# Attention scores with 128 queries of one head on half of TensorE's rows, a bias table of 128 rows, and experts' first matrices laid out anew, in a hybrid mixer and mixture-of-experts kernel

## The chip, the cores and the metric

The kernel runs on one core of one Trainium2 chip. The metric is the device time of one execution in microseconds (us). Below, PE is TensorE's matmuls and PEld its weight loads, DVE is VectorE, ACT ScalarE, POOL GpSimd and SP SyncE, on whose queue most DMAs are issued. A matmul holds a *stationary* operand in the array (loaded ahead of it) and streams a *moving* operand through it; the result goes to a bank of PSUM. In the rows, `64*64` or `128*128` behind a matmul's operands are the rows and columns of the array that it uses, and `64x512 f32` is the moving operand.

## What is computed

One layer of a decoder trunk on 512 tokens of 1024 channels, all in float32 at the ends. The normalised input goes through one projection; 256 channels go through a state-space mixer (S5), 256 through a multi-scale pooling, and 512 through causal attention with 8 heads of 64 channels and a relative bias; the three are joined, go through `w_out` and are added to x. Then each token is sent to two of 16 experts (first a group of four by its logits, then two in the group), and a last norm follows. Cut to what the change touches:

```python
s = einsum('bhqd,bhkd->bhqk', q, k) * dh**-0.5 + bias_t[:, t5_bucket(q_pos - k_pos)]
s = where(q_pos >= k_pos, s, NEG_INF);  out = softmax(s) @ v
x = x + concat([ssm, pool, att]) @ w_out
h = rms_norm(x);  comb = weights of the 2 experts of 16 that each token takes
hg = einsum('td,edf->tef', h, w_gate);  hu = einsum('td,edf->tef', h, w_up)
x = x + einsum('tef,efd->td', silu(hg) * hu * comb, w_down)
```

## The kernel before, in words

The tokens are 4 tiles `m` of 128 (`NT`), the heads 4 pairs `hp` of two (`NPAIR`). The program is written as Python generators (`s_attend`, `s_gather`, `unit_xt` and many more), each a stream of small stages. A stage ends with `yield engine, needs, tokens`: the next stage runs on that engine, after the events `needs`, and holds the `tokens` (buffers). A planner, the class `Flow`, has a cost for every instruction and takes at each step the ready stage that its own clock and the streams' ranks put first. So the order of the instructions on each engine is fixed while the program is built, and the diff does not show it. All instructions are recorded by one helper, so nearly every row of the profile has line L96, and tiles tell the instructions apart.

Attention (`s_attend`, line 1080). For each tile and pair, 64 queries at a time (`b` = 0, 1): two matmuls, one for each head `j`, give the scores `psS`, both into one bank of the tag "at" (there are two such banks), head 0 in partitions 0 to 63 and head 1 in 64 to 127. Then one chain of 128 rows (64 queries of two heads): DVE adds the bias table `tb` and takes the row maximum (`pr<-psS,tb`), ACT takes the exponential, DVE divides, PE transposes (`ptp`), ACT copies the result to `pts`. When both halves are there, `po` multiplies by the values. Scores of tile m have W = 128(m+1) columns.

The bias table `tb` has 64 distances for each of two heads on its 128 partitions, 4 pairs of 576 columns; it is read from a scratch array `t_scr` by 8 DMAs of 16 partitions each (`s_tscr`, near line 777), one long run of a shifted row each. The causal mask is in it.

Routing and experts. When `w_out` for a tile is done, `pth` transposes the normed tile, `pl` gives the router's logits, and DVE, ACT and PE (`pc`, counts of tokens per expert) find each token's slot. Tokens of the first unit of expert work are gathered by matmuls with a 0/1 matrix, `gb<-sel,xp` (`s_gather`, line 1417), whose stationary operand is a 128x128 part of the normed tokens; the other units read their tokens back from memory and transpose them (`tx`, `unit_xt`, line 1595). The 1024 channels are split into 8 parts as `(c k)`: part k takes every eighth channel, so neighbouring columns of an operand are 32 bytes apart. This matches the experts' weights in memory, where a partition holds 8 neighbouring rows. Expert weights arrive as float32, and ACT and DVE split each into two float16 halves (`gu` and `dn`); then `pg` (gate and up) and `py` (down) run on PE.

Of the kernel before, what the change touches and what calls it, by code (L numbers as in the profile page):

```python
# [19 lines left out]
P = 128  # L20
D = 1024
S = 512
# [14 lines left out]
TW = 576  # L37
VW = TW + HD - 1
# [65 lines left out]
class Flow:  # L104
# [176 lines left out]
def hybrid_trunk_kernel(tc, a, out, cap=CAPACITY, dbg=None):  # L281
# [93 lines left out]
    tb = ap_.tile([P, NPAIR, TW], F32, name="tb")  # L375
# [370 lines left out]
    def s_bias():  # L746
# [332 lines left out]
    def s_attend(tiles):  # L1079
        while tiles:  # L1080
            m, hp = tiles.pop(0)
            W = P * (m + 1)
            for b in range(2):
                qt = 2 * m + b
                yield "pe", (("q", hp), ("k", hp), "tb"), ("at",) if b else ("at", "pts")
                if b == 0:
                    pts = ap_.tile([P, NT, 2, P], F32, tag="pts", name=f"pts{m}_{hp}", bufs=2)
# [7 lines left out]
                one = lambda n: ap_.tile([P, 1], F32, tag=n, name=f"{n}{m}_{hp}_{b}", bufs=4)  # L1095
                yield "dve", (), ("pr",)
                pr = ap_.tile([P, S], F32, tag="pr", name=f"pr{m}_{hp}_{b}", bufs=3)
                mx, nm, sm_, rcp = one("mx"), one("nm"), one("smx"), one("rcp")
                v.tensor_tensor_reduce(out=pr[:, 0:W], in0=psS[:, 0:W], in1=tb[:, hp, c0:c0 + W],
                                       scale=1.0, scalar=LOW, op0=ALU.add, op1=ALU.max, accum_out=mx)  # L1100
                fl.give("at")
                v.tensor_scalar(nm, mx, -1.0, None, ALU.mult)
                yield "act"
                act.activation(pr[:, 0:W], pr[:, 0:W], AF.Exp, bias=nm, accum_out=sm_)
                yield "dve"
                v.reciprocal(rcp, sm_)
                v.tensor_scalar(pr[:, 0:W], pr[:, 0:W], rcp, None, ALU.mult)
                yield "pe", (), ("tr",)
                pt = bank("tr", f"ptp{m}_{hp}_{b}")
                for kt_ in range(m + 1):  # L1110
                    pe.transpose(pt[:, kt_ * P:(kt_ + 1) * P], pr[:, kt_ * P:(kt_ + 1) * P], ident)
                fl.give("pr")
                yield "act"
                act.copy(pts[:, 0:m + 1, b, :], pt[:, 0:W].rearrange("p (k q) -> p k q", q=P))
                fl.give("tr")
            yield "pe", tuple(("v", hp // 2, t) for t in range(m + 1)), ("po",)
# [935 lines left out]
```

## Time and profile before

| | us |
|---|---|
| device time, median of 3 runs | 437.32 (436.31, 437.32, 441.03) |
| device time of the profiled run | 435.2 |
| its span | 433.2 |
| mean granted clock of TensorE, as a share | 0.951 |

| engine | busy us | share of the span | instructions |
|---|---|---|---|
| PE | 381.7 | 88% | 3336 |
| PEld (weight loads, beside PE) | 214.4 | 49% | 3336 |
| DVE | 321.1 | 74% | 650 |
| ACT | 236.3 | 55% | 400 |
| POOL | 50.7 | 12% | 86 |

The DMA queues moved 109.41 MB, 253 GB/s in the mean. A row of the timeline gives the start in us from the span's start, the time until the group's last end, engine, line, operation, output and inputs, and behind x the number of instructions in the group; in square brackets stands the idle time just before and what ended it. An f32 matmul is two records in the trace, so `x4` of `psS` are two matmuls.

### The profile page before, as it was taken

Reading aid. Unit: us, or ns where it says so; the run is one execution under the profiler, and the core shown is the slowest. Engines: PE = TensorE matmul, PEld = TensorE weight load, DVE = VectorE, ACT = ScalarE, POOL = GpSimd, SP = SyncE. Lnnn points to the kernel's source line nnn. Section 1 sums busy time; section 2 is a strip of 40 time slices with the busy share of each in tenths; the row PEclk is TensorE's granted clock in tenths of the full one; section 3 lists DMA queues with packets and bytes.
Section 4 is the critical chain, followed back from the end, with each engine's and each line's share of the span. In section 5 each row is a group of like instructions: output and inputs, shape, how many; then the busy total and the mean of one; then the engine's idle time right before and its main releaser. Section 6 shows DMA issues by size and latency. Waiting matters only on the chain. (4 is left out here: it accounts for less than half of the span.)

```text
span 433.2 us, 8564 instructions
## 1 busy us (share of the span) xinstructions
PE 381.7 (88%) x3336; PEld 214.4 (49%) x3336; DVE 321.1 (74%) x650; ACT 236.3 (55%) x400; POOL 50.7 (12%) x86
## 2 busy tenths in 40 slices
PE   2899896898999999999999989899998876678992
PEld 1698453453644465445565975455454432233440
DVE  2798969747368778886898657978888777886383
ACT  4754133335469577865861115846786756466231
POOL 1200003124000000000124620001110010000011
PEclk9999999899999999999999978999998996589997
DMA  8935599219928979765786896548999996989933
GB/s 278 353 109 159 163 162 372 103 23 107 289 93 259 392 252 331 270 219 182 226 308 245 301 422 201 209 132 297 357 378 352 390 309 258 330 277 326 391 131 148
DMA packets 48872, 109.41 MB, mean 253 GB/s; under 512 B 4508, under 2 KB 25756, under 8 KB 48829
## 3 DMA queue, kind: packets, MB, share of 16 engines
q1 hardware_dynamic: 45676, 99.15, 70.0%
q0 software_dynamic: 2592, 9.44, 5.4%
q10 hardware_dynamic: 560, 0.25, 0.4%
q8 instruction: 27, 0.44, 0.4%
q14 instruction: 17, 0.13, 0.1%
HBM read 84.13 MB, written 24.69 MB: 251 GB/s over the span
## 5 line engine op out<-in xcount | busy, mean ns | idle before, releaser
L96 PE MATMUL pg<-gu,xts 128*32 128x512 f16 (+1 forms) x960 | 71.4, 397 | 6.6 <-ACT gu L96 6.6
L96 DVE SCALAR_TENSOR_TENSOR gu<-st_lde,gu 128x1024 f16<-128x1024 f32 x56 | 67.4, 1219 | 11.0 <-ACT gu L96 10.6
L96 ACT ACTIVATE gu<-st_lde 128x1024 f16<-128x1024 f32 x56 | 58.0, 1057 | 18.0 <-DMA st_lde<-in_moe_w_up_dram 10.3
L96 PEld LDWEIGHTS <-xts 128*32 128x32 f16 (+1 forms) x960 | 31.0, 103 | 42.3 <-issue 16.8
L96 PE MATMUL py<-dn,aT 128*32 128x512 f16 (+1 forms) x480 | 40.9, 443 | 6.6 <-ACT aT L96 5.8
L96 PE MATMUL px<-wo,cat 128*128 128x512 f16 x192 | 44.5, 379 | 0.0
L96 DVE SCALAR_TENSOR_TENSOR dn<-st_lde,dn 128x1024 f16<-128x1024 f32 x32 | 38.5, 1220 | 6.3 <-ACT dn L96 6.1
L96 ACT ACTIVATE dn<-st_lde 128x1024 f16<-128x1024 f32 x32 | 33.4, 1058 | 4.3 <-DMA st_lde<-in_moe_w_down_dram 4.2
L96 PEld LDWEIGHTS <-hT 128*64 128x64 f16 (+1 forms) x384 | 31.3, 156 | 5.3 <-issue 1.2
L96 ACT ACTIVATE pr<-pr,nm 128x128 f32<-128x128 f32 (+3 forms) x32 | 17.9, 559 | 22.3 <-DVE nm L96 22.3
L96 PEld LDWEIGHTS <-aT 128*32 128x32 f16 (+1 forms) x480 | 15.3, 109 | 28.6 <-issue 8.9
L96 PEld LDWEIGHTS <-cat 128*128 128x128 f16 x192 | 18.2, 98 | 22.3 <-issue 3.6
L96 DVE CUSTOM_DVE_ANT_0 pr<-psS,tb 128x128 f32<-128x128 f32 (+3 forms) x32 | 15.6, 486 | 14.8 <-PE psS L96 14.7
L96 PE MATMUL ps_v<-w_v,hT 128*128 128x256 f16 x192 | 24.8, 290 | 0.9 <-ACT hT L96 0.5
L96 POOL DMA_INDIRECT y_scr<-ys,tok x10 | 10.5, 1047 | 124.2 <-ACT ys L96 124.2
L96 PE MATMUL psS<-qk 64*64 64x128 f32 (+3 forms) x128 | 23.3, 451 | 0.7 <-ACT qk L96 0.7
L96 PE MATMUL ps_k<-hT,w_k 128*128 128x512 f16 x96 | 22.5, 380 | 0.0
L96 PE MATMUL ps_q<-hT,w_q 128*128 128x512 f16 x96 | 22.2, 380 | 0.0
L96 ACT COPY pts<-ptp 128x128 f32<-128x128 f32 (+3 forms) x32 | 13.1, 422 | 15.4 <-PE ptp L96 15.4
L96 PE MATMUL ptp<-cpk,pr 128*128 128x128 f32 x80 | 14.4, 285 | 7.8 <-DVE pr L96 7.8
L96 POOL TENSOR_TENSOR sm_r<-ss 128x1 f32<-128x1 f32 x4 | 3.6, 901 | 123.0 <-ACT xs L96 123.0
L96 ACT ACTIVATE ys<-py,cw 128x512 f32<-128x512 f32 (+1 forms) x14 | 9.6, 686 | 15.2 <-PE py L96 13.5
(240 smaller groups left out, 653.8 us busy)
## 6 DMA issues: line engine op xcount, KB each, us to landing
st_lde<-in_moe_w_down_dram SPq DMA_DIRECT2D x32, 512.0 KB
st_lde<-in_moe_w_gate_dram SPq DMA_DIRECT2D x28, 512.0 KB
st_lde<-in_moe_w_up_dram SPq DMA_DIRECT2D x28, 512.0 KB
x_scr<-zero SPq DMA_DIRECT2D x12, 512.0 KB
xr<-x_scr SPq DMA_DIRECT2D x10, 512.0 KB
xp<-in_x_dram SPq DMA_DIRECT2D x8, 512.0 KB
y_scr<-zero SPq DMA_DIRECT2D x8, 512.0 KB
yr<-y_scr SPq DMA_DIRECT2D x4, 1024.0 KB
```

Source lines behind the costliest of these rows:

```text
L96: r = f(*args, **kw)
```

## The change

Three things are changed.

First, the scores. The two matmuls of a stage now take 128 queries of one head each, on the array rows of that head (64), all 128 columns, and each writes a bank of its own; the stage takes both "at" banks at once. Then two copies of a new generator `softmax`, one for each head, run the chain that was in the loop, 128 queries of one head each, and `po` waits for the event that the second signals. The number of score matmuls is halved; the chains' instructions keep their numbers and shapes. The planner's cost for a matmul on 64 rows gets a factor of 0.55.

Second, `tb` has 128 distances of one head on its partitions, 8 heads of 512 columns, and is again read by 8 DMAs of 16 partitions. Before, they read 512 runs of 2304 bytes (1.18 MB); now 1024 runs of 2048 bytes (2.10 MB).

Third, the host permutes the rows of the experts' gate and up matrices (`spread`), so that the channels can be split as `(k c)`, part k being 128 neighbouring channels. The loads of the matrices keep their form.

```diff
-TW = 576
-VW = TW + HD - 1
+TW = S
+VW = TW + P - 1
@@ planner's cost of a matmul
+            elif args[1].shape[0] == 64:
+                t *= 0.55
@@ the bias table
-    tb = ap_.tile([P, NPAIR, TW], F32, name="tb")
+    tb = ap_.tile([P, 2 * NPAIR, TW], F32, name="tb")
-        for j in range(2):
-            for r in range(0, HD, NC):
-                sp.dma_start(tb[j * HD + r:j * HD + r + NC], bass.AP(
-                    t_scr.tensor, t_scr.offset + j * NC * (VW + 1) + HD - 1 - r,
-                    [[VW, NC], [2 * NC * (VW + 1), NPAIR], [1, TW]]))
+        for r in range(0, P, NC):
+            sp.dma_start(tb[r:r + NC], bass.AP(
+                t_scr.tensor, t_scr.offset + P - 1 - r,
+                [[VW, NC], [NC * (VW + 1), 2 * NPAIR], [1, TW]]))
@@ s_attend
-            for b in range(2):
-                qt = 2 * m + b
-                yield "pe", (("q", hp), ("k", hp), "tb"), ("at",) if b else ("at", "pts")
...
-                psS = bank("at", f"psS{m}_{hp}_{b}")
-                for j in range(2):
-                    rows = slice(j * HD, (j + 1) * HD)
-                    pe.matmul(psS[rows, 0:W], qk[hp // 2][rows, 0, hp % 2, qt * HD:(qt + 1) * HD],
-                              qk[hp // 2][rows, 1, hp % 2, 0:W],
-                              start=True, stop=True)
-                c0 = 448 - HD * qt
...
+            yield "pe", (("q", hp), ("k", hp), "tb"), ("at", "at", "pts")
+            pts = ap_.tile([P, NT, 2, P], F32, tag="pts", name=f"pts{m}_{hp}", bufs=2)
+            pss = [bank("at", f"psS{m}_{hp}_{j}") for j in range(2)]
+            for j in range(2):
+                rows = slice(j * HD, (j + 1) * HD)
+                pe.matmul(pss[j][:, 0:W], qk[hp // 2][rows, 0, hp % 2, m * P:(m + 1) * P],
+                          qk[hp // 2][rows, 1, hp % 2, 0:W], start=True, stop=True)
+            c0 = TW - W
+            left = [2]
             for b in range(2):
+                fl.spawn(1, softmax(m, hp, b, pss[b], pts, c0, W, left))
+            yield "pe", (("pts", m, hp),) + tuple(("v", hp // 2, t) for t in range(m + 1)), ("po",)
...
-                              pts[:, kt_, :, j * HD:(j + 1) * HD],
+                              pts[:, kt_, j, :],
...
+    def softmax(m, hp, b, psS, pts, c0, W, left):
+        h = 2 * hp + b
...
+        v.tensor_tensor_reduce(out=pr[:, 0:W], in0=psS[:, 0:W], in1=tb[:, h, c0:c0 + W],
+                               scale=1.0, scalar=LOW, op0=ALU.add, op1=ALU.max, accum_out=mx)
+        fl.give("at")
...
+        left[0] -= 1
+        if not left[0]:
+            fl.sig(("pts", m, hp))
@@ s_gather (and the same line in unit_xt and in the path for crowded experts)
-        src = xs_m[m].rearrange("p (c k) -> p k c", k=KD)
+        src = xs_m[m].rearrange("p (k c) -> p k c", k=KD)
@@ host
+    def spread(w):
+        return np.ascontiguousarray(w.reshape(NE, KD, P, FE).transpose(0, 2, 1, 3)).reshape(NE, D, FE)
```

The planner's order moves with it. On PE, in the middle of the attention of pairs 0 and 1, before (`psS_1_1` are the scores of tile and pair's second half, `ptp` the transposes, `po` the product with the values, `pm` the pooling's matmul):

```order
L96 MATMUL ptp_1_0_1134<-cpk,pr_1_0_1089 128x128 x2
L96 MATMUL ptp_1_1_1137<-cpk,pr_1_1_1106 128x128
L96 MATMUL pm_1140<-scr_112,pw_sb 128x512
L96 MATMUL psS_1_1_1143<-qk_117 64x256 x2
L96 MATMUL po_1_1147<-pts_1_1034,v_sb 64x128 x2
L96 MATMUL psS_0_0_1151<-qk_117 64x384 x2
```

and at the same place after the change:

```order
L96 MATMUL po_0_1126<-pts_0_1020,v_sb 64x128 x4
L96 MATMUL ptp_1_0_1131<-cpk,pr_1_0_1084 128x128 x2
L96 MATMUL psS_0_0_1137<-qk_117 128x384
L96 MATMUL psS_0_1_1138<-qk_117 128x384
L96 MATMUL pm_1144<-scr_112,pw_sb 128x512
L96 MATMUL ptp_1_1_1160<-cpk,pr_1_1_1105 128x128 x2
```

The two matmuls of a stage (`x2` before) now stand as two rows with a bank each, next to each other, and the two transposes of a pair lie apart.

At the end of `w_out` for the last tile, on PE, before (`px` is `w_out`, `gb` the gather of two half units for a tile, `pth` the transposes for the router, `pc` the counts):

```order
L96 LDWEIGHTS cat_120
L96 MATMUL px_1_2563<-wo_1_2309,cat_120 128x512
L96 MATMUL gb_2652<-sel,xp_122 128x128 x4
L96 MATMUL gb_2653<-sel,xp_122 128x128 x4
L96 MATMUL pth_1_2676<-cpk,xp_123 128x128 x4
L96 LDWEIGHTS one_89
L96 MATMUL pc_2687<-base_87,one_89 128x16
```

and after:

```order
L96 LDWEIGHTS cat_120
L96 MATMUL px_1_2517<-wo_1_2322,cat_120 128x512
L96 MATMUL gb_2606<-sel,xp_122 128x128 x4
L96 MATMUL pth_1_2619<-cpk,xp_123 128x128 x4
L96 MATMUL gb_2607<-sel,xp_122 128x128 x4
L96 MATMUL gb_2606<-sel,xp_122 128x128 x4
L96 LDWEIGHTS one_89
L96 MATMUL pc_2655<-base_87,one_89 128x16
```

`pth` stands behind four gather matmuls where it stood behind eight, and four more come ahead of the counts. Somewhat later, at the last tile's logits `pl`, before:

```order
L96 MATMUL pc_2687<-hot,tri_88 128x16
L96 MATMUL gb_2652<-sel,xp_122 128x128 x4
L96 MATMUL pl_2708<-rw,h2T_2618 128x20 x8
L96 MATMUL gb_2653<-sel,xp_122 128x128 x4
L96 MATMUL gb_2652<-sel,xp_123 128x128 x4
L96 MATMUL gb_2653<-sel,xp_123 128x128 x4
L96 LDWEIGHTS one_89
L96 MATMUL pc_2762<-base_87,one_89 128x16
```

and after:

```order
L96 MATMUL pc_2655<-hot,tri_88 128x16
L96 MATMUL pl_2663<-rw,h2T_2573 128x20 x8
L96 MATMUL gb_2607<-sel,xp_122 128x128 x4
L96 MATMUL gb_2606<-sel,xp_123 128x128 x4
L96 MATMUL gb_2607<-sel,xp_123 128x128 x4
L96 LDWEIGHTS one_89
L96 MATMUL pc_2716<-base_87,one_89 128x16
```

The logits no longer stand behind a gather; the same three gathers lie between them and the last counts.

## Rows read from the trace of the kernel before

**Rows 1.** Windows by stage: stretch, its us, engines' busy time, clock, DMA share, GB/s

```profile
65.60:205.60 140.00, 131.98 (x879) 68.29 (x879) 101.97 (x246) 85.92 (x178) 13.83 (x16) 0.99 0.73 222
205.60:258.85 53.25, 50.56 (x296) 37.03 (x295) 40.40 (x138) 19.48 (x32) 17.81 (x33) 0.94 0.83 297
340.00:433.00 93.00, 68.60 (x638) 30.28 (x634) 63.24 (x85) 46.07 (x68) 6.41 (x9) 0.87 0.78 280
```

**Rows 2.** The tile of scores: ns of one (min/median/max), starts, forms

```profile
L96 PE MATMUL psS<-qk x128: 269/454/641, 65.7 to 198.6; 64*64 64x128 f32 x32, 64*64 64x256 f32 x32, 64*64 64x384 f32 x32, 64*64 64x512 f32 x32
```

**Rows 3.** Timeline of PE in the attention: scores, and other matmuls for comparison

```profile
97.92 0.86 PE L96 MATMUL psS<-qk 64*64 64x384 f32 x4
98.72 1.47 PE L96 MATMUL ps_p<-hT,w_p 128*128 128x512 f16 x6
...
119.25 1.08 PE L96 MATMUL psS<-qk 64*64 64x512 f32 x4
120.25 1.47 PE L96 MATMUL ps_q<-hT,w_q 128*128 128x512 f16 x6
...
126.29 1.88 PE L96 MATMUL pz<-xp,xs 128*128 128x512 f32 x4
128.10 1.08 PE L96 MATMUL psS<-qk 64*64 64x512 f32 x4
```

**Rows 4.** Timeline from the last tile's `w_out` to the first expert matmuls

```profile
237.82 3.89 PE L96 MATMUL gb<-sel,xp 128*128 128x128 f32 x16
238.66 0.68 DVE L96 SCALAR_TENSOR_TENSOR xp<-px,xp 128x512 f32<-128x512 f32 x1
241.55 0.60 PE L96 MATMUL pth<-cpk,xp 128*128 128x128 f32 x4
244.35 1.86 PE L96 MATMUL pl<-rw,h2T 128*128 128x20 f32 x16
249.49 0.23 DVE L96 TENSOR_SCALAR hot<-sm_r 128x16 f16<-128x16 f32 x1
252.05 0.18 PE L96 MATMUL pc<-base,one 1*128 1x16 f16 x1
254.83 4.09 PE L96 MATMUL gb<-sel,xs 128*128 128x128 f32 x16 [2.11 <-DVE sel L96]
258.85 5.36 PE L96 MATMUL pg<-gu,xts 128*32 128x512 f16 x96
```

**Rows 5.** Groups by line and form: f32 weight loads, busy us, mean ns of one

```profile
L96 PEld LDWEIGHTS gb<-sel,xp 128*128 128x128 f32 x48 | 11.8, 335 | 0.1
L96 PEld LDWEIGHTS tx<-cpk,xr 128*128 128x128 f32 x80 | 10.0, 194 | 5.8 <-issue 3.4 <-DVE xts L96 2.1 <-DVE dn L96 0.4
L96 PEld LDWEIGHTS ptp<-cpk,pr 128*128 128x128 f32 x80 | 9.3, 141 | 15.9 <-DVE pr L96 7.8 <-issue 5.1 <-ACT cat L96 0.7
...
L96 PEld LDWEIGHTS pl<-rw,h2T 128*128 128x128 f32 x64 | 7.6, 192 | 0.1
```

**Rows 6.** Timeline around the first use of the bias table

```profile
52.38 4.02 SPq L96 DMA_DIRECT2D tb<-t_scr  x8
...
69.91 0.28 DVE L96 CUSTOM_DVE_ANT_0 pr<-psS,tb 128x128 f32<-128x128 f32 x1
...
77.81 0.48 PE L96 MATMUL ptp<-cpk,pr 128*128 128x128 f32 x1 [4.70 <-DVE pr L96]
```

**Rows 7.** Windows, columns as in Rows 1, while the bias table loads and after

```profile
56.00:64.00 8.00, 8.00 (x97) 5.09 (x96) 5.30 (x5) 3.56 (x5) 0.00 (x0) 1.00 1.06 130
64.00:72.00 8.00, 7.31 (x39) 3.22 (x38) 7.96 (x13) 2.51 (x5) 0.35 (x2) 1.00 1.09 359
```

**Rows 8.** Page, part 5: score reductions and expert splits on DVE

```profile
L96 DVE SCALAR_TENSOR_TENSOR gu<-st_lde,gu 128x1024 f16<-128x1024 f32 x56 | 67.4, 1219 | 11.0 <-ACT gu L96 10.6
...
L96 DVE CUSTOM_DVE_ANT_0 pr<-psS,tb 128x128 f32<-128x128 f32 (+3 forms) x32 | 15.6, 486 | 14.8 <-PE psS L96 14.7
```

**Rows 9.** Timeline: the first split of later experts' weights

```profile
267.32 1.99 ACT L96 ACTIVATE gu<-raw 128x1024 f16<-128x1024 f32 x2
```

More of the change, by code (lines that the diff above doesn't have):

```diff
@@ L1082, in s_attend @@
             W = P * (m + 1)
-            for b in range(2):
-                qt = 2 * m + b
-                yield "pe", (("q", hp), ("k", hp), "tb"), ("at",) if b else ("at", "pts")
-                if b == 0:
-                    pts = ap_.tile([P, NT, 2, P], F32, tag="pts", name=f"pts{m}_{hp}", bufs=2)
-                psS = bank("at", f"psS{m}_{hp}_{b}")
-                for j in range(2):
-                    rows = slice(j * HD, (j + 1) * HD)
-                    pe.matmul(psS[rows, 0:W], qk[hp // 2][rows, 0, hp % 2, qt * HD:(qt + 1) * HD],
-                              qk[hp // 2][rows, 1, hp % 2, 0:W],
-                              start=True, stop=True)
-                c0 = 448 - HD * qt
[L1095 to L1115, printed above, removed]
@@ L1116, in s_attend @@
-            yield "pe", tuple(("v", hp // 2, t) for t in range(m + 1)), ("po",)
+            yield "pe", (("q", hp), ("k", hp), "tb"), ("at", "at", "pts")
[5 more added lines that the diff above has]
+                          qk[hp // 2][rows, 1, hp % 2, 0:W], start=True, stop=True)
@@ L1128, in s_attend @@
             fl.sig(("att", m, hp))
+    def softmax(m, hp, b, psS, pts, c0, W, left):
+        h = 2 * hp + b
+        one = lambda n: ap_.tile([P, 1], F32, tag=n, name=f"{n}{m}_{hp}_{b}", bufs=4)
+        yield "dve", (), ("pr",)
+        pr = ap_.tile([P, S], F32, tag="pr", name=f"pr{m}_{hp}_{b}", bufs=3)
+        mx, nm, sm_, rcp = one("mx"), one("nm"), one("smx"), one("rcp")
+        v.tensor_tensor_reduce(out=pr[:, 0:W], in0=psS[:, 0:W], in1=tb[:, h, c0:c0 + W],
+                               scale=1.0, scalar=LOW, op0=ALU.add, op1=ALU.max, accum_out=mx)
+        fl.give("at")
+        v.tensor_scalar(nm, mx, -1.0, None, ALU.mult)
+        yield "act"
+        act.activation(pr[:, 0:W], pr[:, 0:W], AF.Exp, bias=nm, accum_out=sm_)
+        yield "dve"
+        v.reciprocal(rcp, sm_)
+        v.tensor_scalar(pr[:, 0:W], pr[:, 0:W], rcp, None, ALU.mult)
+        yield "pe", (), ("tr",)
+        pt = bank("tr", f"ptp{m}_{hp}_{b}")
+        for kt_ in range(m + 1):
+            pe.transpose(pt[:, kt_ * P:(kt_ + 1) * P], pr[:, kt_ * P:(kt_ + 1) * P], ident)
+        fl.give("pr")
+        yield "act"
+        act.copy(pts[:, 0:m + 1, b, :], pt[:, 0:W].rearrange("p (k q) -> p k q", q=P))
+        fl.give("tr")
+        left[0] -= 1
+        if not left[0]:
+            fl.sig(("pts", m, hp))
     ATT = tuple(("att", m, hp) for m in range(NT) for hp in range(NPAIR))
@@ L1596, in unit_xt @@
         left = [2]
-        src = xr.rearrange("p (c k) -> p k c", k=KD)
+        src = xr.rearrange("p (k c) -> p k c", k=KD)
         for h in range(2):
@@ L1922, in hybrid_trunk_kernel @@
                     pt = psF.tile([P, 512], F32, tag="pf", name=f"pf{t}_{k}")
-                    pe.transpose(pt[:, 0:P], hs.rearrange("p (c k) -> p k c", k=KD)[:, k], ident)
+                    pe.transpose(pt[:, 0:P], hs.rearrange("p (k c) -> p k c", k=KD)[:, k], ident)
                     v.tensor_copy(hTf[:, k, t * P:(t + 1) * P], pt[:, 0:P])
@@ L1979, in layouts @@
          "w_in": f["w_in"].reshape(D, NPROJ), "w_out": f["w_out"].reshape(D, D),
-         "moe_w_gate": f["moe_w_gate"].reshape(NE, D, FE), "moe_w_up": f["moe_w_up"].reshape(NE, D, FE),
+         "moe_w_gate": spread(f["moe_w_gate"]), "moe_w_up": spread(f["moe_w_up"]),
          "moe_w_down": f["moe_w_down"].reshape(NE, FE, D)}
```

## The prediction, made before the change was run

> **What bounds the kernel now.** I read the windows by stage first, since a busy share over the whole span mixes stages with different limits. In [rows 1] the reader is to see PE's busy time against the length of each stretch. From the first scores (65.6 us) to the end of the attention's neighbourhood (205.6) PE is busy 131.98 of 140.00 us, 94%, at a clock of 0.99; from there to the first expert matmuls (258.85) it is busy 50.56 of 53.25, 95%. DVE and ACT have room in both. So up to 258.85 time taken out of PE's row of instructions moves everything behind it forward. In the last stretch PE is busy 68.60 of 93.00 us, so there it waits for something else, and a faster PE buys little. The chain of work that ended last covers only the last two microseconds and says nothing on this. Then I read the tile of the scores, the timeline of PE, and the groups by form.
>
> **A. Scores, in the first stretch.** There are 32 f32 records of each of four widths [rows 2]; four records are one stage (two matmuls of two records each), so 8 stages per width. From the start of a group to that of the next, four records of 384 columns take 98.72-97.92 = 0.80 us, and of 512 columns 120.25-119.25 = 1.00 us [rows 3]. The step of 0.20 per 128 columns gives 0.60 and 0.40 for the two smaller widths: (0.40+0.60+0.80+1.00) x 8 = 22.4 us in all. The change leaves 4 stages per width instead of 8, each with the same four records and the same moving columns.
>
> What does one stage then cost? Four records of 512 columns over the whole array (`pz`) take 128.10-126.29 = 1.81 us [rows 3], nearly twice the 1.00 of the scores. So the two heads' matmuls run side by side today. They use different rows and different columns of the array; after, they use different rows but the same columns, each with a bank of its own. If they still run side by side, the scores cost 22.4/2 = 11.2 and the change saves 11.2 us. If not, they go at the rate of `pz`: 1.81 x (1+2+3+4)/4 x 4 = 18.1, and it saves 4.3. No row shows two half-height matmuls over the same columns. The nearest is `psS` itself, whose heads differ in rows too, so I take the side near it: **10 us**, a little under the full gain since the weight loads are now 128 columns wide.
>
> **B. Gather and routing, in the second stretch.** The gather's stationary operand changes from every eighth channel to neighbouring ones. Its weight load takes 335 ns, where `pl`, of the same form from neighbouring elements, takes 192; among transposes, strided `tx` takes 194 and contiguous `ptp` 141 [rows 5]. So the stride lengthens a load. In `gb` the pace is 3.89/16 = 0.243 us a record, in `pl` 1.86/16 = 0.116 [rows 4]; a matmul of 128 moving columns alone needs 1.81/16 = 0.113 by `pz` [rows 3]. I take 0.12 us a record; 0.243 is the other bound (no gain). In `tx` the load grows by only 53 ns against `ptp`, and a load lies beside the matmul before it, so I count no gain there.
>
> Not all 64 records are on the path, so I follow it [rows 4]. `pth` starts at 241.55, behind 16 gather records; after, it stands behind 8, which end by 237.82+8x0.12 = 238.8, and its input is written by DVE at 238.66+0.68 = 239.34. So it starts near 239.4, 2.15 earlier, and the logits `pl` at 242.2 instead of 244.35. The one-hot `hot` ends at 249.72, 3.51 after the logits' end (246.21); now 242.2+1.86+3.51 = 247.57. The 24 gather records between now end by 247, so the counts `pc` start near 247.7 instead of 252.05: 4.35 earlier. The last gather follows 2.78 later, at 250.5, and its 16 records take 1.95 instead of 4.02, so the expert matmuls `pg` could start near 252.5 instead of 258.85. Their second half needs a cast behind the gather's end, which costs a few tenths. I take **6 us** (0 to 6.4).
>
> **C. The bias table.** It grows from 1.18 to 2.10 MB. While it loads, the DMA engines are fully busy (share 1.06) and move only 130 GB/s; once it is in, the same share moves 359 [rows 7]. At 130 GB/s, 2.10 MB take 16.1 us instead of 9.1. Its issues begin at 52.38; with a start-up of about 2 it then lands near 71, and its first reader starts at 69.91 [rows 6]. DVE is busy 7.96 of 8.00 us there [rows 7], so a late table delays it one for one, and PE, which already waits 4.70 us for DVE at 77.81 [rows 6], with it. The loads of projection weights behind the table come later as well. From below it costs 0 (it lands in time), from above the whole 7.0. I take **2.5 us lost**, since the estimate lies one to two microseconds behind the first use. [...]
>
> **D. Both score banks at once.** A stage now needs both "at" banks, so PE can't write a pair's scores while the other half is being reduced. DVE's 32 reductions take 486 ns in the mean, and DVE waits 14.7 us in all for PE's scores [rows 8]: today the scores, not the banks, are late. The bounds are 0 and one reduction for each of the 16 pairs, 16 x 0.486 = 7.8. I take **1 us lost**, since PE has other matmuls to run meanwhile.
>
> **E. What costs nothing.** Products with the values, transposes, exponentials and copies keep number and shape; a contiguous moving operand for `po` changes no row that I can find. The rows of the experts' matrices are permuted on the host, and their DMAs keep their form. What the late stage waits for are experts' weights. The splits of the weights that were loaded early begin at 267.32, with the first units of expert work [rows 9], and free the buffers of the next loads. These move forward with PE, so the gain should carry through; I add 0. If they did not, it would be swallowed, which is a rival below.
>
> **Sum.** 10 + 6 - 2.5 - 1 = 12.5 us. The profiled run took 435.2, so 422.7 by the same measure. The median of the runs is 2.1 above that run, so the forecast for the median is **425**.
>
> **The rivals.**
> 1. *The heads no longer run side by side.* Same columns of the array, so one after the other at the rate of `pz`: 4.3 + 6 - 3.5 = 6.8 us saved, about 430.5. Against it: the rows differ, as they do now.
> 2. *The end stage swallows it.* If the experts' weights arrive when they arrived before, because DMA sets their time (share 0.78 and 280 GB/s in the last stretch, where PE is idle a quarter of the time [rows 1]), the early gain turns into waiting: 435 to 438. Against it: the loads' buffers are freed by splits that start with PE's progress [rows 9].
> 3. *Slower: the pairs run in lockstep.* The chains of a pair start together, and the next scores need both banks. If each time the second reduction waits behind one weight split on DVE (1219 ns) and takes its own 486 ns [rows 8], and PE, its order fixed, stands still behind it, each of 16 pairs costs 1.7 us, 27 in all, against 16 saved less 2.5 by the table: 437.3+13.9 = about 451. It decides from (16-2.5)/16 = 0.84 us a pair on; the time is over 1% longer from 1.12. For it: DVE carries splits between the attention's instructions. Against it: DVE is busy only 102 of 140 us in that stretch [rows 1], and PE has projections and state-space matmuls between the pairs.
> 4. *Everything at its good end.* 11.2 + 6.4 and no loss: 17.6, so about 420.
>
> **How the numbers follow.** Forecast 0.58, rival 1 0.13, rival 2 0.15, rival 3 0.09, rival 4 0.05. The predicted time is that of the forecast. The range reaches down to 418, just under rival 4, and up to 434, over rival 1, and leaves out rivals 2 and 3 (0.24 together, of which the range's edge takes back a little). A change of 1%, 4.4 us, is about what a measurement of this kernel can tell from none. Forecast, rivals 1 and 4 are faster by more: 0.76, of which I give 0.02 to no change, since D and C together at their dear ends would eat rival 1; so faster 0.74, same 0.17 (rival 2 and this), slower 0.09.
>
> **What would show it.** A: four score records of 512 columns still take about 1.00 us from start to start, with 64 `psS` records instead of 128; if they take 1.8, rival 1 holds. B: `gb` at 0.12 us a record with a weight load near 192 ns, and from the last `pth` to the first `pg` about 13 us instead of 17.3. C: the first `pr<-psS,tb` one to three microseconds later against the scores ahead of it, with a wait for a DMA. D: no wait of PE's scores for DVE's reductions above some tenths; many of 1 to 2 us are rival 3. E: the distance from the first `pg` to the end unchanged at 433.2-258.85 = 174 us; if it grows by ten, rival 2 holds. I would be wrong above all if the planner's new order leaves PE waiting at places where it was fed before, which the rows of before can't show.

## The result, and the profile after

| | before | changed |
|---|---|---|
| device time, median of 20 runs, us | 437.45 | 432.8 |
| ratio to before, with its 95% interval | | 0.9889 (0.9864 to 0.9914) |
| span of the profiled run, us | 433.2 | 429.4 |
| mean granted clock of TensorE | 0.951 | 0.949 |

The change makes the kernel faster by 1.1%, 4.65 us between the medians. The forecast was 425, 12.4 us less than before: the sign is right, the size is not. Ratios, here and below, compare the fast runs alone, while times are medians of all runs, so the two can differ by some microseconds.

Four stretches tell where. The timeline of the changed kernel (start, us, engine, line, operation, output and inputs, idle time before):

```profile
73.81 0.29 DVE L96 CUSTOM_DVE_ANT_0 pr<-psS,tb 128x128 f32<-128x128 f32 x1 [3.79 <-DMA xs<-in_glu_w_dram]
...
81.37 0.28 DVE L96 TENSOR_SCALAR pr<-pr,rcp 128x128 f32<-128x128 f32 x1
...
81.71 0.48 PE L96 MATMUL ptp<-cpk,pr 128*128 128x128 f32 x1 [8.95 <-DVE pr L96]
...
88.80 0.70 PE L96 MATMUL psS<-qk 64*128 64x256 f32 x4
89.43 0.41 PE L96 MATMUL pk<-s1b,bbd 128*32 128x128 f32 x2
...
98.51 0.92 PE L96 MATMUL psS<-qk 64*128 64x384 f32 x4
99.35 1.13 PE L96 MATMUL pm<-scr,pw_sb 128*128 128x512 f32 x2
...
108.14 1.13 PE L96 MATMUL psS<-qk 64*128 64x512 f32 x4
109.20 0.55 PE L96 MATMUL ptp<-cpk,pr 128*128 128x128 f32 x3
...
207.01 0.59 PE L96 MATMUL px<-wo,cat 128*128 128x512 f16 x2 [1.77 <-ACT wo L96]
208.27 5.16 PE L96 MATMUL px<-wo,cat 128*128 128x512 f16 x16 [0.67 <-DVE wo L96]
...
236.01 1.05 PE L96 MATMUL gb<-sel,xp 128*128 128x128 f32 x8
236.97 0.66 PE L96 MATMUL pth<-cpk,xp 128*128 128x128 f32 x4
237.46 1.95 PE L96 MATMUL gb<-sel,xp 128*128 128x128 f32 x16
...
245.40 0.18 PE L96 MATMUL pc<-base,one 1*128 1x16 f16 x1
...
248.63 3.50 PE L96 MATMUL gb<-sel,xs 128*128 128x128 f32 x16 [2.56 <-DVE sel L96]
253.53 5.36 PE L96 MATMUL pg<-gu,xts 128*32 128x512 f16 x96 [1.40 <-DVE xts L96]
```

The first row's wait is for the bias table: the trace puts it down to another DMA, but with a faster table it is gone, and the kernel before with a larger table has the same wait with `tb` named (both below). The first scores start at 65.69 us, as before. From there:

| from ... to | before | changed | gain | forecast |
|---|---|---|---|---|
| first scores ... first transposes `ptp` | 77.81 [rows 6] | 81.71 | -3.9 | -2.5 (C) |
| ... first gather `gb` of the last block | 237.82 [rows 4], 160.0 later | 236.01, 154.3 later | 5.7 | 9 (A, D) |
| ... first expert matmul `pg` | 258.85 [rows 4], 21.0 later | 253.53, 17.5 later | 3.5 | 6 (B) |
| ... end | 433.2, 174.3 later | 429.4, 175.9 later | -1.5 | 0 (E) |
| sum | | | 3.8 | 12.5 |

Each of the four came out worse than forecast, and none by enough to explain the miss alone. The windows of the changed kernel (columns as in rows 1):

```profile
82.00:100.00 18.00, 18.00 (x106) 9.95 (x106) 11.94 (x44) 7.50 (x27) 3.20 (x4) 0.91 0.58 183
100.00:140.00 40.00, 38.19 (x294) 20.65 (x293) 27.55 (x65) 26.60 (x50) 6.31 (x6) 1.00 0.71 164
...
205.00:235.00 30.00, 27.56 (x162) 16.54 (x160) 21.12 (x68) 15.46 (x24) 8.76 (x16) 0.94 0.69 239
...
81.70:236.20 154.50, 148.87 (x968) 83.60 (x969) 112.91 (x300) 96.43 (x196) 18.27 (x26) 0.98 0.72 222
...
248.60:251.00 2.40, 2.37 (x12) 2.37 (x13) 1.88 (x8) 0.54 (x2) 1.85 (x4) 0.58 1.01 413
```

and of the kernel before, the stretches that answer to 81.70:236.20 and to the last gather:

```profile
77.80:238.00 160.20, 156.35 (x1028) 83.87 (x1028) 117.63 (x306) 99.95 (x199) 17.50 (x26) 0.99 0.71 218
...
254.80:258.90 4.10, 4.07 (x20) 3.95 (x24) 2.50 (x16) 0.81 (x2) 1.21 (x4) 0.61 1.02 417
```

PE has only 7.5 us less to do there (156.35 against 148.87), although the scores save 10 (below): the clock is 0.91 behind the wait for the table and 0.94 around the waits for `w_out`'s weights, and other matmuls take longer there. In 82:100 those of `ps_p` take 424 ns in the mean, in 205:235 those of `px` 401; in the same windows of before, at a clock of 1.00, they take 380 and 379. And it idles 5.6 us instead of 3.9; the waits for `w_out`'s weights, 1.77 and 0.67 us, do not stand in the trace of before.

### The profile page after: what moved, and what is told of

Same layout as the page of the kernel before. It is cut to its first block, busy times and chain, and to the rows that moved or that the text cites. A ratio compares the mean times of both kernels' runs of the same rounds, so it can differ in the third digit from the quotient of the medians.

```text
span 429.4 us, 8450 instructions
## 1 busy us (share of the span) xinstructions
PE 364.4 (85%) x3272; PEld 204.9 (48%) x3272; DVE 321.7 (75%) x649; ACT 236.1 (55%) x400; POOL 54.6 (13%) x87
## 4 chain that ended last, share of the span: by engine, by line
PE 50%; DMA 24%; DVE 13%; ACT 5%; issue 4%; SPq 1%; POOL 0%; POOLq 0%; ACTq 0%; DVEq 0%
PE px L96 7%; DMA st_lde<-in_moe_w_down_dram 7%; PE pg L96 6%; PE py L96 5%; DMA st_lde<-in_moe_w_gate_dram 4%; PE pf L96 4%; PE ps_v L96 4%; DVE gu L96 4%; DMA st_lde<-in_moe_w_up_dram 4%; DMA xs<-in_glu_w_dram 3%; PE psS L96 3%; PE pu L96 3%; PE ptp L96 3%; PE ps_k L96 3%; DVE dn L96 2%
## 5 line engine op out<-in xcount | busy, mean ns | idle before, releaser
L96 DVE SCALAR_TENSOR_TENSOR gu<-st_lde,gu 128x1024 f16<-128x1024 f32 x55 | 68.0, 1251 | 15.9 <-ACT gu L96 15.6
L96 PE MATMUL pg<-gu,xts 128*32 128x512 f16 (+1 forms) x960 | 71.7, 395 | 8.6 <-ACT gu L96 7.2
L96 ACT ACTIVATE gu<-st_lde 128x1024 f16<-128x1024 f32 x56 | 58.2, 1056 | 16.4 <-DMA st_lde<-in_moe_w_up_dram 11.1
L96 PEld LDWEIGHTS <-xts 128*32 128x32 f16 (+1 forms) x960 | 31.1, 103 | 44.0 <-issue 20.4
L96 PE MATMUL px<-wo,cat 128*128 128x512 f16 x192 | 45.6, 389 | 2.4 <-ACT wo L96 1.8
L96 PE MATMUL py<-dn,aT 128*32 128x512 f16 (+1 forms) x480 | 39.0, 420 | 8.8 <-ACT aT L96 7.5
L96 DVE SCALAR_TENSOR_TENSOR dn<-st_lde,dn 128x1024 f16<-128x1024 f32 x32 | 38.6, 1218 | 2.4 <-ACT dn L96 1.8
L96 ACT ACTIVATE dn<-st_lde 128x1024 f16<-128x1024 f32 x32 | 33.2, 1053 | 7.6 <-DMA st_lde<-in_moe_w_down_dram 7.5
L96 PEld LDWEIGHTS <-hT 128*64 128x64 f16 (+1 forms) x384 | 30.7, 155 | 5.1 <-issue 1.4
L96 PEld LDWEIGHTS <-cat 128*128 128x128 f16 x192 | 18.9, 100 | 24.3 <-issue 6.0
L96 PEld LDWEIGHTS <-aT 128*32 128x32 f16 (+1 forms) x480 | 14.8, 105 | 30.1 <-ACT aT L96 9.7
L96 ACT ACTIVATE pr<-pr,nm 128x128 f32<-128x128 f32 (+3 forms) x32 | 17.9, 562 | 15.0 <-DVE nm L96 14.8
L96 POOL DMA_INDIRECT y_scr<-ys,tok x10 | 11.9, 1190 | 103.9 <-ACT ys L96 78.6
L96 PE MATMUL ps_v<-w_v,hT 128*128 128x256 f16 x192 | 24.1, 282 | 1.0 <-ACT hT L96 0.6
L96 PE MATMUL ps_q<-hT,w_q 128*128 128x512 f16 x96 | 22.6, 380 | 0.0
L96 PE MATMUL ps_k<-hT,w_k 128*128 128x512 f16 x96 | 22.2, 380 | 0.0
L96 PE MATMUL ptp<-cpk,pr 128*128 128x128 f32 x80 | 13.6, 284 | 9.5 <-DVE pr L96 9.3
L96 DVE CUSTOM_DVE_ANT_0 pr<-psS,tb 128x128 f32<-128x128 f32 (+3 forms) x32 | 15.5, 485 | 7.7 <-DMA xs<-in_glu_w_dram 3.8
L96 ACT COPY pts<-ptp 128x128 f32<-128x128 f32 (+3 forms) x32 | 12.7, 424 | 12.5 <-PE ptp L96 12.4
L96 PEld LDWEIGHTS ptp<-cpk,pr 128*128 128x128 f32 x80 | 9.2, 141 | 17.4 <-DVE pr L96 9.4
L96 ACT ACTIVATE xs<-xp 128x512 f32<-128x512 f32 (+1 forms) x12 | 9.2, 770 | 14.5 <-DVE xp L96 10.7
L96 DVE TENSOR_TENSOR xts<-tx,xts 128x512 f16<-128x512 f32 x22 | 14.7, 685 | 2.4 <-ACT xts L96 2.1
```

What stands on the lines that cost most here:

```text
L96: r = f(*args, **kw)
```

## Experiments: the bias table

All ratios are to the kernel before, run on the same chip beside each of them. A difference to the changed kernel is given between the medians, which come from different chips, and in brackets by the ratios, where 1% is 4.4 us.

**The table on partitions 8 apart.** The same 2.10 MB in 1024 runs of the same length, but each DMA writes partitions r, r+8, r+16, ... instead of 16 neighbours. It reads each row from another of the 16 copies in `t_scr`, so the starts of its runs lie 2528 bytes apart instead of 2556:

```diff
-        for r in range(0, P, NC):
-            sp.dma_start(tb[r:r + NC], bass.AP(
+        for r in range(P // NC):
+            sp.dma_start(tb[r:P:P // NC], bass.AP(
                 t_scr.tensor, t_scr.offset + P - 1 - r,
-                [[VW, NC], [NC * (VW + 1), 2 * NPAIR], [1, TW]]))
+                [[VW + 1 - P // NC, NC], [NC * (VW + 1), 2 * NPAIR], [1, TW]]))
```

> The changed kernel with the same bias table, loaded by 8 DMAs of 16 partitions that lie 8 apart instead of side by side. Theory (the late table costs about 4 us, and the transfer is slow because 16 neighbouring partitions are written at a time): the first reduction of scores starts near 70 instead of 73.8, PE's wait for the first transposes falls from 8.95 to about 5 us, and the time falls by 3 to 4 us to a ratio of about 0.98 to before. Rival 1 (the partitions don't matter, the transfer is bound by the size or number of its runs): first reduction still near 73.8, ratio 0.989. Rival 2 (the table comes earlier but w_out's last weights still arrive near 207, so the gain is waited away): first reduction near 70, ratio 0.989.

Measured: 428.1 us, ratio 0.9788 (0.9752 to 0.9824), 4.7 us less than the changed kernel's median (4.4). Windows of each while the table loads, first the changed kernel, then this one:

```profile
56.00:60.00 4.00, 4.00 (x23) 2.29 (x22) 1.35 (x2) 2.98 (x4) 0.00 (x0) 1.00 1.10 128
60.00:64.00 4.00, 4.00 (x76) 2.79 (x75) 3.93 (x4) 0.59 (x1) 0.00 (x0) 1.00 1.07 124
```

```profile
56.00:60.00 4.00, 4.00 (x23) 2.29 (x22) 1.36 (x2) 2.97 (x4) 0.00 (x0) 1.00 1.06 205
60.00:64.00 4.00, 4.00 (x76) 2.79 (x75) 3.93 (x4) 0.59 (x1) 0.00 (x0) 1.00 1.08 207
```

and the timeline of this one:

```profile
69.92 0.28 DVE L96 CUSTOM_DVE_ANT_0 pr<-psS,tb 128x128 f32<-128x128 f32 x1
...
77.82 0.47 PE L96 MATMUL ptp<-cpk,pr 128*128 128x128 f32 x1 [5.07 <-DVE pr L96]
```

With the DMA engines as busy, 205 to 207 GB/s flow instead of 124 to 128. The first reduction starts at 69.92, as before the change (69.91, [rows 6]), and the first transposes at 77.82. The late table is thus real and costs 3.9 us at this place and 4.4 to 4.7 at the end. Both rivals of this run fall. The way from the one place to the other isn't shown: the traced execution is the longest of the five (433.6 us, the others 426 to 428), its mean clock is 0.936 where the changed kernel's is 0.949, and its gather starts at 237.83, later than the changed kernel's. Whether the partitions alone or also the other starts of the runs make the table faster was not tested apart.

**The larger table alone, in the kernel before.** Each run of a row is 1024 columns long instead of 576, of which the kernel uses 576; the planner counts the old size, so the order of all engines is that of before (one DMA of 2 KB more fills the end of `t_scr`):

```diff
-    tb = ap_.tile([P, NPAIR, TW], F32, name="tb")
+    tb = ap_.tile([P, NPAIR, 1024], F32, name="tb")
...
-                    [[VW, NC], [2 * NC * (VW + 1), NPAIR], [1, TW]]))
+                    [[VW, NC], [2 * NC * (VW + 1), NPAIR], [1, 1024]]))
```

> The kernel before with its own order and table, but 1024 instead of 576 columns loaded of each row (2.10 MB instead of 1.18, the rest of a row is not used). Theory (the larger table alone costs about 4 us and a lower clock behind the wait): first reduction of scores 3 to 4 us later, ratio about 1.01. Rival (the table's lateness is caught up later): first reduction later, ratio 1.00.

Measured: 440.4 us, ratio 1.006 (1.0015 to 1.0106), 2.5 us more. Its timeline:

```profile
74.07 0.29 DVE L96 CUSTOM_DVE_ANT_0 pr<-psS,tb 128x128 f32<-128x128 f32 x1 [3.88 <-DMA tb<-t_scr]
```

DVE waits 3.88 us, where the changed kernel waits 3.79, and 2.5 of it are left at the end. The larger table alone makes a kernel slower, between the two cases that were expected.

**The clock behind the wait.** 34 matmuls of 512 columns without use, put on PE where it waits for the table:

```diff
         pt = bank("tr", f"ptp{m}_{hp}_{b}")
+        if not warm:
+            warm.append(1)
+            for _ in range(34):
+                nc.tensor.matmul(pt, hT[0][:, 0, 0:P], hT[0][:, 0, :], start=True, stop=True)
```

> The changed kernel with 34 matmuls of 512 columns without use put on PE where it waits for the late table (72.8 to 81.7): the wait and everything else stay, but TensorE's clock should not fall behind it. Theory (the clock's fall after the wait, 0.91 in the stretch 82 to 100, costs 2 to 3 us of the saving): the stretch behind the wait at clock 1.00, w_out ends 2 us earlier, ratio 0.984 to 0.986. Rival (the clock there is caught up later): ratio 0.989.

Measured: 429.5 us, ratio 0.9808 (0.9762 to 0.9853), 3.3 us less than the changed kernel's median (3.5). The timeline and two windows of it:

```profile
72.95 7.50 PE L1131 MATMUL ptp<-hT 128*128 128x512 f16 x34
80.44 0.33 PE L96 MATMUL ptp<-cpk,pr 128*128 128x128 f32 x1
```

```profile
82.00:100.00 18.00, 18.00 (x117) 10.19 (x115) 12.99 (x50) 9.15 (x31) 3.32 (x5) 1.00 0.55 162
100.00:140.00 40.00, 37.75 (x277) 20.19 (x276) 26.80 (x57) 26.83 (x46) 6.21 (x5) 0.96 0.75 178
```

The stretch behind the wait now runs at 1.00 instead of 0.91. That stretch lost about 18.0 x 0.09 = 1.6 us of full-speed work. But the next 40 us run at 0.96 instead of 1.00, which is 1.6 us again: from the first transposes to the gather (80.44 to 234.90) this trace needs 154.5 us, the changed kernel's 154.3. The first transposes come at 80.44 instead of 81.71. So the run is faster, but its trace doesn't show that the clock is why; the cause of the 3.3 us stays open.

**The planner told of the price.** In the planner's cost of a DMA, 16 partitions go at 130 GB/s:

```diff
-        return 0.35, _bytes(out) / 360e3
+        return 0.35, _bytes(out) / (130e3 if out.shape[0] == 16 else 360e3)
```

> The changed kernel, but the planner prices a DMA to 16 partitions at 130 GB/s instead of 360, so that it knows when the table really lands and sets the order of all engines by it; the transfer itself is as in the changed kernel. Theory (the order put scores' first reduction, and all of DVE's state-space work behind it, in front of a table that isn't there): DVE no longer waits 3.8 us for it, PE's wait of 8.95 us shrinks to 5 or less, ratio about 0.98. Rival (what is moved ahead is missing later, the stages behind set the time): ratio 0.989.

Measured: 425.4 us, ratio 0.9666 (0.9608 to 0.9723), the fastest kernel of this study. PE's timeline:

```profile
73.53 0.49 PE L96 MATMUL psS<-qk 64*128 64x128 f32 x4
73.95 0.41 PE L96 MATMUL pk<-s1b,bbd 128*32 128x128 f32 x2
78.30 0.41 PE L96 MATMUL pk<-s,bbd 128*32 128x128 f32 x2 [3.93 <-DVE s L96]
...
229.97 1.05 PE L96 MATMUL gb<-sel,xp 128*128 128x128 f32 x8
...
246.55 5.36 PE L96 MATMUL pg<-gu,xts 128*32 128x512 f16 x96
```

The scores now start at 73.53, eight microseconds later, and DVE doesn't stand behind the table. The gather starts at 229.97, 6.0 us earlier than in the changed kernel. The gain is larger than the theory's.

The same price in the kernel before, where the table lands in time:

> The kernel before, only with the planner pricing a DMA to 16 partitions at 130 GB/s instead of 360. If the gain that the changed kernel took from this price (0.989 to 0.967) is the late table's, the kernel before, in which the table lands before its first use, gains nothing: ratio 1.00 (0.995 to 1.005). If it is a better order in general, the kernel before gains as much: 0.98.

Measured: 441.7 us, ratio 1.0119 (1.008 to 1.0158), which neither case expected. So the price isn't a better order in general; there it makes a worse one. And the price together with the partitions 8 apart (200 GB/s):

> Both at once: the table loaded to partitions 8 apart (about 205 GB/s in the trace of that run) and priced by the planner at 200 GB/s. If the table no longer stands in the way once it is loaded so, the price changes little: ratio 0.979 as with the faster table alone. If PE's remaining wait of some 5 us before the first transposes is also the table's: 0.97.

Measured: 435.8 us, ratio 0.996 (0.9928 to 0.9991), worse than either alone, which neither case expected. PE's waits between 66 and 240 us (total, times, longest):

```profile
PE px L96 <- ACT wo L96: 7.9, 1, 7.9
PE psS L96 <- DVE mx L96: 4.9, 2, 4.5
```

In this order `w_out`'s last weights come 7.9 us too late. Each of these three runs draws a new order of everything, and an order can be a per cent better or worse for a reason far from the edit. What they show surely is only what their rows show.

## Experiments: the layout, and the scores alone

**The layout undone, and done alone.** The third part taken out of the changed kernel, and put alone into the kernel before; no instruction changes its place by it. The first of the two, cut (the same line changes in `unit_xt` and in the path for crowded experts):

```diff
-        src = xs_m[m].rearrange("p (k c) -> p k c", k=KD)
+        src = xs_m[m].rearrange("p (c k) -> p k c", k=KD)
...
     def spread(w):
...
-        return np.ascontiguousarray(w.reshape(NE, KD, P, FE).transpose(0, 2, 1, 3)).reshape(NE, D, FE)
+        return w.reshape(NE, D, FE)
```

> The changed kernel with the third part undone: channels split as every eighth again, experts' matrices as before. Theory (from the end of w_out to the first expert matmul the layout is worth 20.9-17.4 = 3.5 us, and this carries through): gather records at 0.24 to 0.25 us again, time 3 to 4 us longer, ratio about 0.997. Rival (the experts' weights set the end, the layout is worth nothing there): the first expert matmul comes 3.5 us later, ratio 0.989 all the same. If my prediction's 6 us held, ratio 1.003.

> The kernel before with only the third part of the change (layout of the experts' first matrices and split of the channels). Theory: 3.5 us of gain between the end of w_out and the first expert matmul, ratio 0.992. Rival (expert weights set the end): ratio 1.00. Prediction's 6 us: ratio 0.986.

Measured: undone 440.7 us, ratio 1.010 (1.0068 to 1.0133), which is 7.9 us above the changed kernel's median (9.2) and slower than before; alone 435.1 us, ratio 0.9863 (0.9812 to 0.9914), which is 6.0 us by the ratio and 2.9 us between the medians. So the layout undone costs more than any of the three cases expected, and the layout alone is worth 3 to 6 us, which doesn't decide between 3.5 and 6. Without the layout the changed kernel is 1.0% slower than before: in this order the layout carries the whole gain. Groups by form, first of the kernel with the layout undone, then of the changed one:

```profile
L96 PEld LDWEIGHTS gb<-sel,xp 128*128 128x128 f32 x48 | 11.8, 335 | 0.4 <-DVE sel L96 0.2
L96 PEld LDWEIGHTS gb<-sel,xs 128*128 128x128 f32 x16 | 3.9, 335 | 2.2 <-DVE sel L96 2.2
```

```profile
L96 PEld LDWEIGHTS gb<-sel,xp 128*128 128x128 f32 x48 | 5.8, 192 | 1.2 <-DVE sel L96 1.1
...
L96 PEld LDWEIGHTS gb<-sel,xs 128*128 128x128 f32 x16 | 3.2, 306 | 2.7 <-DVE sel L96 2.7
```

The weight load falls from 335 to 192 ns, as forecast, but not in the last 16 (306): there the clock is 0.58, behind PE's wait of 2.56 us for `sel`.

**Scores alone, with two orders.** The layout undone together with the table 8 partitions apart, and together with the planner's price:

> Scores part alone, without the price of the table: the changed kernel with the channels split as before (third part undone) and the table loaded to partitions 8 apart. Theory (the 10.6 us of PE time that the scores save are given back before the end, since experts' weights set the pace of the last stage and their splits now crowd the routing): ratio to before about 1.00. Rival (the late table is the only loss): the saved time shows, ratio about 0.98.

Measured: 434.7 us, ratio 0.9925 (0.9871 to 0.998), between the theory and the rival.

> Scores part with the priced table and the channels split as before (third part undone). Theory (with the table out of the way most of the scores' saving shows, and the layout is worth 3.5 to 8 us on top of it): ratio 0.980 to 0.985 against 0.967 with the layout. Rival (as in the run with the table 8 partitions apart, the saving is given back at the experts): 0.99 to 1.00.

Measured: 429.6 us, ratio 0.9834 (0.9742 to 0.9926), 4.2 us above the same kernel with the layout (7.3), as the theory expected. Against the kernel before, the scores part without the layout gives 3 us with the faster table and 7 with the price, which also draws a new order; with the table late it loses 2.6 (4.4 by the ratio; undone, above). The layout's direct gain, from the first gather to the first expert matmul, is nearly the same in four pairs of kernels without and with it (table at the end of the next section): 4.8 to 5.7 us. At the end, by medians and ratios, the same four pairs give 2.9 to 6.0, 7.9 to 9.2, 6.0 to 6.6 and 4.2 to 7.3.

## Experiments: where PE's time goes

**PE's time given back.** Every score matmul issued twice, all else in its order:

```diff
+                nc.tensor.matmul(pss[j][:, 0:W], qk[hp // 2][rows, 0, hp % 2, m * P:(m + 1) * P],
+                                 qk[hp // 2][rows, 1, hp % 2, 0:W], start=True, stop=True)
+            for j in range(2):
+                rows = slice(j * HD, (j + 1) * HD)
                 pe.matmul(pss[j][:, 0:W], qk[hp // 2][rows, 0, hp % 2, m * P:(m + 1) * P],
```

> The changed kernel with every score matmul issued twice, everything else in the same order: PE gets back the 10.6 to 12 us of busy time that the scores part saves, and nothing else changes. Theory (PE time in the attention is worth little): 0 to 3 us longer than the changed kernel, ratio 0.989 to 0.996. Rival (PE sets the pace up to the routing and the gain was lost in other ways): 9 to 12 us longer, ratio about 1.012.

Measured: 437.3 us, ratio 0.9961 (0.9908 to 1.0014), 4.5 us above the changed kernel's median (3.1). Its timeline, the second copies under line L96, and a window:

```profile
112.42 1.02 PE L96 MATMUL psS<-qk 64*128 64x512 f32 x4
113.38 0.55 PE L96 MATMUL ptp<-cpk,pr 128*128 128x128 f32 x3
...
243.44 1.05 PE L96 MATMUL gb<-sel,xp 128*128 128x128 f32 x8
260.75 5.36 PE L96 MATMUL pg<-gu,xts 128*32 128x512 f16 x96 [1.40 <-DVE xts L96]
```

```profile
205.00:243.40 38.40, 36.24 (x208) 20.85 (x207) 30.29 (x79) 22.02 (x33) 8.75 (x16) 1.00 0.73 251
```

The second copies take 0.32, 0.53, 0.75 and 0.96 us from start to start for the four widths, 10.2 us in all. The gather comes 7.4 us later than in the changed kernel, 1.1 of it by a later first transpose (82.79), and the first expert matmul 7.2 later, but the end only 3.1 to 5.2 (by ratios, medians and spans, 434.6 and 429.4). So of 10 us of PE time in the attention, some two thirds reach the experts and three to five tenths the end. This lies between theory and rival. It is not quite the same kernel with more to do: around the waits for `w_out`'s weights the clock is 1.00 here and 0.94 in the changed kernel, about 30.0 x 0.06 = 1.8 us of full-speed work that the copies don't cost.

**Fewer bytes at the end.** The second half of the down matrices of experts 8 to 15 isn't loaded; the splits read the first half twice:

```diff
+                if e >= 8 and i == 2 and j == 1:
+                    continue
                 yield "sp", need, ("stg", "fly")
                 stage_load(("lde", e, i, j), [source(e, i, j)], [1, D] if i == 2 else [4, FE])
+                if e >= 8 and i == 2:
+                    staged["lde", e, 2, 1] = staged["lde", e, 2, 0]
+                    fl.sig_dma(("lde", e, 2, 1))
...
```

> The changed kernel without the second half of the down matrices of experts 8 to 15: 8 of 512 KB loads are left out and the splits read the first half twice, so 4.2 MB less are loaded in the last stage and all computation stays. Theory (the loads of experts' weights set the pace from the first unit on): 8 to 11 us shorter than the changed kernel, ratio about 0.968. Rival (the splits on ACT and DVE, or PE, set it): within 3 us of the changed kernel, ratio about 0.985.

Measured: 421.5 us, ratio 0.960 (0.9489 to 0.971), 11.3 us less than the changed kernel's median (12.6, with an uncertainty of some 5), as the theory expected. In its trace the first expert matmul starts at 256.13, later than the changed kernel's 253.53, and the end follows 163.8 us behind it instead of 175.9. 4.2 MB in 12.1 us are 347 GB/s, near the rate that the windows of the changed kernel show there:

```profile
280.00:300.00 20.00, 20.00 (x293) 9.92 (x292) 17.44 (x21) 14.17 (x21) 4.04 (x4) 1.00 0.58 198
300.00:320.00 20.00, 19.46 (x236) 9.07 (x232) 15.77 (x20) 13.06 (x19) 2.50 (x4) 1.00 1.00 379
320.00:340.00 20.00, 20.00 (x268) 10.26 (x266) 17.04 (x21) 15.00 (x22) 3.56 (x6) 1.00 0.99 365
```

From 300 to 340 us the DMA engines are full (share 1.00 and 0.99). I read this so that the end is set by how early this stream of weights starts and by what keeps it from flowing; a hole is left at 280 to 300 (share 0.58). No run moved the stream's start alone.

**`w_out`'s last weights earlier.** Their loads wait for an earlier expert's load, eight places up in SP's queue:

```diff
-                need = ((("att", NT - 1, 1),) if kk < 2 else (("lde", 3, 0, 1),)) if nh else (("start", "q1"),)
+                need = ((("att", NT - 1, 1),) if kk < 2 else (("lde", 2, 0, 1),)) if nh else (("start", "q1"),)
```

> The changed kernel with the last two loads of w_out's weights eight places earlier in SP's queue (they wait for an earlier expert's load). Theory (PE reaches w_out's last quarter before its weights, and waits some 3 us at 205 to 208): the waits of w_out's matmuls for wo (1.77 and 0.67 us) go, w_out ends 2 to 4 us earlier, ratio about 0.981. Rival (the wait only moves: buffers are held longer, so experts' weights come later): w_out ends earlier, but the time stays at 0.989 or gets worse.

Measured: 432.8 us, ratio 0.9893 (0.9852 to 0.9935), no change. The timeline:

```profile
234.15 1.95 PE L96 MATMUL gb<-sel,xp 128*128 128x128 f32 x16
...
243.16 3.78 PE L96 MATMUL gb<-sel,xp 128*128 128x128 f32 x16 [2.79 <-DVE sel L96]
...
254.85 7.28 PE L96 MATMUL pg<-gu,xts 128*32 128x512 f16 x96 [1.40 <-DVE xts L96]
```

The gather starts 1.9 us earlier and the first expert matmul 1.3 later: the wait went into the routing, where PE now waits 2.79 us for `sel`, and the 16 gather records behind that wait take 3.78 us, where those at 234.15 take 1.95. The time is the rival's; its reason, later weights, isn't what this trace shows.

**The traces side by side.** Starts in us; each row is one execution, and executions of one kernel differ by several us (the changed kernel's 20 run from 428.2 to 437.6):

| kernel | first gather | to `pg` | first `pg` | `pg` to the end |
|---|---|---|---|---|
| before | 237.82 | 21.0 | 258.85 | 174.4 |
| before, layout alone | 239.45 | 16.2 | 255.64 | 177.7 |
| before, larger table | 242.78 | 21.4 | 264.15 | 173.0 |
| changed | 236.01 | 17.5 | 253.53 | 175.9 |
| changed, layout undone | 236.94 | 22.8 | 259.77 | 178.2 |
| changed, table spread | 237.83 | 17.6 | 255.47 | 176.3 |
| the same, layout undone | 235.00 | 23.4 | 258.36 | 174.1 |
| changed, price | 229.97 | 16.6 | 246.55 | 178.6 |
| the same, layout undone | 230.77 | 21.4 | 252.13 | 173.6 |
| changed, scores twice | 243.44 | 17.3 | 260.75 | 173.9 |
| changed, `w_out`'s weights earlier | 234.15 | 20.7 | 254.85 | 173.0 |
| changed, fewer bytes | 237.55 | 18.6 | 256.13 | 163.8 |

The first expert matmul starts anywhere from 246.55 to 264.15, and the end follows 173 to 179 us behind it wherever all weights are loaded.

## Why the prediction was wrong, step by step

**A, the scores: the mechanism and the saving on PE were right, their worth was not.** Two heads on half of the rows do run side by side over the same columns. From start to start, four records take 89.43-88.80 = 0.63 us for 256 columns, 99.35-98.51 = 0.84 for 384 and 109.20-108.14 = 1.06 for 512, against 0.80 and 1.00 for the two larger widths before [rows 3]; with the smaller widths of both traces (0.42 after, 0.36 and 0.58 before) the scores take 11.8 us instead of 22.0. So 10 us are saved where 10 were forecast, though the weight loads of the scores, 128 columns wide instead of 64, take 192 ns in the mean instead of 131. Rival 1 falls. The step that failed is the first one: "up to 258.85 time taken out of PE's row of instructions moves everything behind it forward". From the first transposes to the gather the changed kernel needs 5.7 us less, where A and D had 9: the clock falls to 0.91 behind the table and to 0.94 around `w_out`'s weights (1.00 in both windows before), and PE waits for those weights where it was fed before, which the prediction's last sentence had named as its danger. PE was 94% busy, but it was not alone in setting the pace. Given back by the doubled matmuls, the saved time costs three to five tenths of itself at the end. A, C and D together had 6.5 us of gain; measured without the layout, they lose 2.6 to 4.4. How much of A's loss is the clock's and how much the waits' stays open.

**E, what costs nothing: nearly right.** The forecast let the whole gain through to the end and put the distance from the first `pg` to the end at an unchanged 174 us. It is 175.9, so 1.5 of the 5.3 us that `pg` gained were lost, and rival 2, whose sign was a growth by ten, falls. In the traces side by side the end follows `pg` at 173 to 179 us however early `pg` comes. With the layout and the price, `pg` comes 12.3 us earlier than before (246.55 against 258.85) and the end 8.1 (spans 425.1 and 433.2). But the same order without the layout gives 173.6, so a loss of a third is no more than traces differ by. Whether some of the gain is swallowed isn't shown. The run with fewer bytes shows that the loads have a large part in this stage's length: it is 163.8 us there.

**C, the table: mis-sized, and passed on as forecast.** The table did land late, and DVE did wait. The forecast landing near 71 was too early: windows of one us stay at 113 to 142 GB/s from 68 to 72 and show 294 in the next, and the first reduction starts at 73.81. The start-up of 2 us in it was an estimate; the trace of before has a figure near it: the write of `t_scr`, 320 KB, is issued at 50.15, and the table's DMAs, which wait for it, follow at 52.38, 2.23 later, the transfer included. Start-up and transfer, 18.1 us in the forecast, took some 20, from the first issue at 52.38 to the step in these windows. So 2.5 us became 3.9 at the place and 4.4 to 4.7 at the end by the faster table. The delay went on one for one, as forecast: 73.81-69.91 = 3.90 at the reduction and 81.71-77.81 = 3.90 at the transposes. Left out was the clock of 0.91 behind PE's wait (1.00 in the same window before), a wait that rose from 4.70 to 8.95. With the partitions of a DMA 8 apart, 205 to 207 GB/s flowed instead of 124 to 128, other transfers counted in.

**B, the layout: the size was about right, the way there was not.** The pace is 1.95/16 = 0.122 us a record, as forecast. `pth` to the first `pg` fell from 17.3 to 16.6 only, though the forecast had 13. Up to the experts the layout gives 4.8 to 5.7 us in four pairs, and at the end 3 to 9, against 6; why the end can gain more than the place isn't shown. Two terms of the path were left out: the last 16 records run at a clock of 0.58 (3.50 us instead of 1.95), and `pg` then waits 1.40 us for its last cast. That wait of 1.40 us comes with the changed kernel's order: it stands in its trace with the layout undone too, and makes up most of the 1.8 us by which that kernel's stretch is longer than the one of before (22.8 against 21.0).

**D, both banks at once:** the changed kernel's scores wait for DVE only twice, in their weight loads (total, times, longest), so under 1 us:

```profile
PEld psS L96 <- DVE rcp L96: 0.4, 1, 0.4
PEld psS L96 <- DVE nm L96: 0.4, 1, 0.4
```

Rival 3, the lockstep, falls for this order; in the order with the price and the spread partitions the scores do wait for a row maximum, 4.9 us in two waits.

## What to carry to other kernels

A busy share of 94% says that an engine is a bound, not that it is the only one. Before a saving on it is counted in full, ask what the other engines and the DMA queues do in its shadow, and whether the engine will find its next operands there when it comes earlier; a run that gives the saved time back on that engine measures its worth, though it moves waits and the clock as well. A table that is needed early is worth a run with spread partitions (205 to 207 GB/s instead of 124 to 128 here). A planner's price moves the whole order (ratios 0.967, 1.012 and 0.996 here), so it has to be run with each kernel anew. And one trace is one execution: differences of 2 us between two traces say little without the times of several runs.

## What the runs showed of the hardware

- A table loaded by DMAs to 16 neighbouring partitions each came at 124 to 128 GB/s, with all DMA engines busy (share 1.07 to 1.10); by DMAs to 16 partitions 8 apart, in runs of the same 2048 bytes, at 205 to 207 (share 1.06 to 1.08; windows above, other transfers counted in).
- The strided f32 weight load of the gather took 335 ns in the first 48 records and 335 in the last 16, whose stretch had a clock of 0.61 before the change (window 254.80:258.90 above), and its pace hardly differed (0.243 and 4.09/16 = 0.256 us, [rows 4]). The contiguous load took 192 ns at a clock of 1.00 (236 to 246 us) and 306 in the mean of the last 16, with a pace of 0.122 us, and 3.50/16 = 0.219 at a clock of 0.58. So undoing the stride saved 1.94 us of 16 records at full clock (3.89 less 1.95) and 0.59 where the clock was down (4.09 less 3.50).
- Two matmuls on the two halves of the rows, over all columns and with a bank each, overlapped almost fully: 1.06 us for two of 512 columns, 0.06 more than when they shared no column, where two on the whole array took 1.81 [rows 3].
